# Rotated scan states in one operation, the gated product of the S5 branch in fp32, and four score banks, in a hybrid decoder block

## The chip, the cores and the metric

The kernel runs on one core of a Trainium2 chip. The metric is the device time of one execution in microseconds (us), the median over runs. The engines of the core run side by side, each through its own list of instructions in the order of that list: PE (TensorE, matrix products into PSUM banks), DVE (VectorE), ACT (ScalarE), POOL (GpSimd) and SP (SyncE, here only transfers). They wait for each other through semaphores.

## The reference

One decoder layer on 512 tokens of width 1024. The mixer in its middle has two branches, of which the change touches the second and the front of the first:

```
h = h + 1/2 * SwiGLU_1(RMSNorm(h))
z = RMSNorm(h) @ W_in      # queries, keys, values, branch gates, S5 input u
o = concat(NSA(8 heads x 64), S5(32 groups x 16 channels)) @ W_out
h = h + o
h = h + 1/2 * SwiGLU_2(RMSNorm(h))
h = h + sigmoid(RMSNorm(h) @ W_gate) * (p @ W_ple)
out = RMSNorm(h)

# S5, complex state of 64 for each group:
bu    = (u @ b) * b_coef
state = scan over time of  s[t] = a_bar * s[t-1] + bu[t]
y     = Re(state) @ c_re - Im(state) @ c_im + d_skip * u
y     = gelu(y)
out   = y * sigmoid(y @ w_glu + b_glu)

# NSA: three attentions (compressed, selected and window blocks), mixed by gates
```

## The kernel before

All data is fp32. Most matrix products are made from halves: a factor is split into a rounded part `hi` (a cast on ACT, L147) and a rest `lo` (a subtraction on DVE, L149), and three fast products `xh*hi + xl*hi + xh*lo` replace one fp32 product (`mm3`). `oh` and `ol` are the two halves of the input of `W_out`. The weights come in units of 128x1024 numbers (`raw<-in_wpack`, issued on ACT's queue into a ring of four buffers).

The program is FFN1 (to about 390 us, with `s5_constants` in the background on DVE and POOL), the mixer, and FFN2 with the last gate. In the mixer the S5 scan runs in time blocks of 8, so a group has 64 steps. It is cut into 8 chunks `j` of 4 groups (GC=4). For each chunk, `s5_in` loads the constants `sc`, multiplies the input into bank `w` (PE), turns the result by a complex rotation (L788 to L791, DVE), scans (L794), and turns the states back (L797 to L802) into `xx`, shifted by one step. `s5_out` multiplies `u` and `xx` by further constants into bank `y`, where the two groups of a pair stand at partitions 0 and 64, and ACT copies `y` out (L816). After every second chunk `s5_back` transposes eight 64-token pieces and ACT copies them to `yt` (L826). There are four `yt`, one for every 128 channels. `glu` first runs `gelu2` on each `yt` (ACT square, DVE, ACT tanh, DVE: L744 to L752) and then the product with `w_glu`.

Beside the S5 chunks stand, in the order in which a timeline simulator in the build lays them out on each engine: `scores` of query blocks 3 and 2 (16 groups each: two products and a mask into bank B, the row maximum `nmax` on DVE, the exponential on ACT), the compressed keys and values (`cmp_kv`, `cmp_all`: 32 fp32 products of width 256, `KAc`, `KBc`, `VLc`), the gates, the `glu`, `compressed(3, 2)` (the scores on compressed keys, 16 small pairs of products for each block), and the products of `out_half(4..8)` with `W_out` (96 split products) that fill gaps from there on. The hand-written part of the order is the code of the mixer's end (L1201 to L1208). After about 566 us the values phase follows, in which no line of the change stands.

The queries come through `qf` (SP's queue) as three halves: `QA` upper part (ACT, L1035), `QA` lower part (DVE, L1037), and `QB` (DVE, L1036; its rows 64 to 112 are written with zeros by an ACT cast of 1.04 us, L1039).

Of the kernel before, what the change touches and what calls it, by code (L numbers as in the profile page):

```python
# [10 lines left out]
F32 = mybir.dt.float32  # L11
# [65 lines left out]
def block_kernel(ctx: ExitStack, tc: tile.TileContext, a: dict, out: bass.AP):  # L77
# [341 lines left out]
    s5d = dram.tile([128, NG, 512], F32, tag="s5d", name="s5d")  # L419
    fd, md, gd, cd, sd = (s5d[:, :, i:j] for i, j in ((0, 128), (128, 256), (256, 384), (384, 448), (448, 512)))  # L420
    r8 = pers.tile([128, NG], F32, name="r8")

    def s5_constants(sp):
        yield 3
        if True:
# [175 lines left out]
            nc.gpsimd.dma_start(gd, gt[:, :, 1:9, :].rearrange("p g k o -> p g (k o)"))  # L601

# [86 lines left out]
    def mixer(ctx):  # L689
# [89 lines left out]

        def s5_in(j):  # L780
            sc = s5w.tile([128, GC, 512], F32, tag="sc", name="sc", bufs=3)
            G.dma_start(sc, s5d[:, GC * j:GC * j + GC])
            co, si = sc[:, :, 384:448], sc[:, :, 448:512]
            w = bank(TW, (128, GC, 64))
            for g in range(GC):
                mm(w[:, g], sc[:, g, 0:128], u8[:, GC * j + g], True, True)
            t1, t2 = (s5w.tile([128, GC, 64], F32, tag=n, name=n) for n in ("t1", "t2"))
# [8 lines left out]
            x1, x2 = (s5w.tile([128, GC, 64], F32, tag=n, name=n) for n in ("t1", "t2"))  # L796
            V.tensor_tensor(x2[64:128], vv[0:64], si[0:64], OP.mult)  # L797
            V.tensor_tensor(x2[0:64], vv[64:128], si[64:128], OP.mult)
            V.tensor_tensor(x1, vv, co, OP.mult)
            xx = s5w.tile([128, GC, 64], F32, tag="xx", name="xx")  # L800
            G.memset(xx[:, :, 0:1], 0.0)
            V.tensor_tensor(xx[:, :, 1:64], x1[:, :, 0:63], x2[:, :, 0:63], OP.add)  # L802
            return sc, xx

        def s5_out(j, yc, sc, xx):
# [12 lines left out]
        def s5_back(m, yc):  # L818
            p = bank(TP, (128, 8, 64))
            for t in range(8):  # L820
                PE.transpose(p[:, t], yc[:, t], ident[:64, :64])
# [4 lines left out]
            S.copy(yt, p.rearrange("p t c -> p (t c)"))  # L826
# [150 lines left out]

# [524 lines left out]
```

## Time and profile before

| what | value |
| --- | --- |
| median of 3 runs | 1079.37 us (1076.33 to 1081.54) |
| profiled execution | 1077.02 us, of which the span of the trace is 1075.2 us |
| granted TensorE clock, mean | 0.988 |
| busy: PE, DVE, ACT, POOL | 1038.5, 775.6, 462.3, 162.8 us |

The profiled execution is one further run, 2.35 us below the median of the three. The 1.8 us between its time and its span lie before the first and after the last instruction. Ends of matrix products are modelled, so products that follow each other closely overlap in the rows; what one costs is the distance from its start to the next start. In the rows of a timeline "x4" means four records merged; an fp32 product leaves two records.

### The profile page before, as it was taken

To read this page: it belongs to the slowest core of one execution; us is meant where nothing else is said; L and a number is where in the kernel's file an instruction comes from. 1 tells how busy PE (TensorE), PEld (TensorE's weight loads), DVE (VectorE), ACT (ScalarE), POOL (GpSimd) and SP (SyncE) were. 2 spreads that over 40 slices of the span, in tenths; PEclk is the share of its full clock that TensorE was granted. 3 is DMA by queue.
4 is the path that set the end of the run, shared out by engine and by line. 5 is a ranking of instruction groups with operands and counts; after the bars stand their busy time and mean duration, and the time that the engine had idled before them with its cause. 6 is when DMAs were issued, how large, how long until landed. Compare 5 with 4: busy or idle time off the path is not lost.

```text
span 1075.2 us, 15120 instructions
## 1 busy us (share of the span) xinstructions
PE 1038.5 (97%) x5854; PEld 879.3 (82%) x5854; DVE 775.6 (72%) x1328; ACT 462.3 (43%) x786; POOL 162.8 (15%) x187
## 2 busy tenths in 40 slices
PE   7999999999999999998899999999999999999995
PEld 5888888888888888865687667899899899898895
DVE  6995454545447857889688977996598588687766
ACT  6222223124222523346859865654255246255541
POOL 4006065425629300000000000000000000000000
PEclk9999999999999999999799999999999999999998
DMA  7333335335833837866120014333233423325402
GB/s 258 118 99 102 94 98 156 104 94 175 176 98 111 282 111 219 227 195 226 40 78 21 1 40 137 99 118 118 79 119 107 129 77 101 118 80 162 131 3 79
DMA packets 48696, 128.48 MB, mean 119 GB/s; under 512 B 10400, under 2 KB 17152, under 8 KB 47600
## 3 DMA queue, kind: packets, MB, share of 16 engines
q10 hardware_dynamic: 26080, 90.51, 27.0%
q0 software_dynamic: 4336, 17.60, 6.2%
q1 hardware_dynamic: 18208, 19.40, 5.8%
q8 instruction: 46, 0.75, 0.3%
q14 instruction: 26, 0.21, 0.1%
HBM read 111.99 MB, written 15.73 MB: 119 GB/s over the span
## 4 chain that ended last, share of the span: by engine, by line
PE 82%; DVE 8%; issue 4%; ACT 4%; DMA 2%; POOLq 0%; POOL 0%; DVEq 0%; SPq 0%; ACTq 0%
PE ps_C L126 24%; PE ps_A L126 24%; PE ps_B L126 22%; PE ps_D L126 11%; DVE nmax L1055 1%; DVE lo L149 1%; ACT e L744 1%; DMA raw<-in_wpack 1%; DMA cst<-vcd 1%; ACT eh L744 1%; ACT ps_B L744 1%; DVE el L1150 0%; ACT oh L998 0%; DVE QA L1037 0%; DVE vv L794 0%
## 5 line engine op out<-in xcount | busy, mean ns | idle before, releaser
L147 ACT CAST hi<-raw 128x1024 fp32r<-128x1024 f32 (+2 forms) x148 | 153.8, 1042 | 346.8 <-PE ps_C L126 125.0
L149 DVE TENSOR_TENSOR lo<-raw,hi 128x1024 fp32r<-128x1024 f32 (+2 forms) x148 | 191.1, 1294 | 53.4 <-ACT hi L147 52.8
L126 PE MATMUL ps_C<-hq,hi 128*128 128x512 f32 x704 | 217.3, 390 | 0.7 <-DVE h L404 0.7
L126 PEld LDWEIGHTS ps_C<-hq,hi 128*128 128x128 f32 x704 | 131.5, 188 | 28.2 <-DVE h L404 1.5
L126 PE MATMUL ps_A<-xh,hi 128*128 128x512 f32 (+1 forms) x376 | 132.6, 353 | 7.2 <-ACT xh L170 6.3
L126 PE MATMUL ps_C<-hq,lo 128*128 128x512 f32 x352 | 137.0, 389 | 0.0
L126 PE MATMUL ps_A<-xl,hi 128*128 128x512 f32 (+1 forms) x376 | 132.7, 353 | 0.9 <-DVE xl L222 0.8
L126 PE MATMUL ps_A<-xh,lo 128*128 128x512 f32 (+1 forms) x376 | 131.9, 351 | 1.7 <-DVE lo L149 1.7
L126 PE MATMUL ps_B<-xh,hi 128*128 128x512 f32 (+1 forms) x280 | 102.7, 367 | 0.9 <-ACT hi L147 0.9
L126 PE MATMUL ps_B<-xh,lo 128*128 128x512 f32 (+1 forms) x280 | 102.7, 367 | 0.0
L126 PE MATMUL ps_B<-xl,hi 128*128 128x512 f32 (+1 forms) x280 | 102.3, 365 | 0.0
L264 POOL TENSOR_TENSOR ri<-ms,negh 128x4 f32<-128x4 f32 (+1 forms) x6 | 5.5, 920 | 582.8 <-DVE ms L263 582.8
L126 PEld LDWEIGHTS ps_A<-xh,hi 128*128 128x128 f32 x376 | 71.5, 190 | 17.4 <-ACT xh L170 6.3
L404 DVE SCALAR_TENSOR_TENSOR h<-ps_C,h 128x512 f32<-128x512 f32 x64 | 43.9, 689 | 55.4 <-PE ps_C L126 55.4
L126 PEld LDWEIGHTS ps_A<-xl,hi 128*128 128x128 f32 x376 | 71.4, 190 | 12.6 <-DVE xl L222 2.4
L126 PEld LDWEIGHTS ps_A<-xh,lo 128*128 128x128 f32 x376 | 71.5, 190 | 11.0 <-DVE lo L149 1.9
L147 ACT CAST hi<-s 128x1024 fp32r<-128x1024 f32 x40 | 42.1, 1053 | 86.8 <-PE ps_D L126 37.6
L126 PEld LDWEIGHTS ps_C<-hq,lo 128*128 128x128 f32 x352 | 66.1, 188 | 13.7
L149 DVE TENSOR_TENSOR lo<-s,hi 128x1024 fp32r<-128x1024 f32 x40 | 49.0, 1225 | 16.5 <-ACT hi L147 16.4
L126 PEld LDWEIGHTS ps_B<-xh,hi 128*128 128x128 f32 x280 | 52.7, 188 | 10.0 <-ACT hi L147 1.3
L126 PEld LDWEIGHTS ps_B<-xh,lo 128*128 128x128 f32 x280 | 52.7, 188 | 9.0 <-DVE lo L149 0.4
L126 PEld LDWEIGHTS ps_B<-xl,hi 128*128 128x128 f32 x280 | 52.7, 188 | 8.7 <-issue 0.2
(402 smaller groups left out, 2311.0 us busy)
## 6 DMA issues: line engine op xcount, KB each, us to landing
raw<-in_wpack ACTq DMA_DIRECT2D x168, 512.0 KB, 3.6
sc<-s5d POOLq DMA_DIRECT2D x8, 1024.0 KB, 7.5
raw<-in_wpack SPq DMA_DIRECT2D x4, 512.0 KB, 7.3
h<-in_xT SPq DMA_DIRECT2D x8, 256.0 KB, 4.9
s5d<-fs POOLq DMA_DIRECT2D x1, 2048.0 KB, 11.6
s5d<-gt POOLq DMA_DIRECT2D x1, 2048.0 KB, 13.7
s5d<-tcs POOLq DMA_DIRECT2D x2, 1024.0 KB, 9.3
qf<-qd SPq DMA_DIRECT2D x16, 128.0 KB, 3.1
```

What stands on the lines that cost most here:

```text
L126: return PE.matmul(o, lhsT, rhs, start=start, stop=stop, **kw)
L147: S.copy(hi[:, c], raw[:, c])
L149: V.tensor_tensor(lo[:, c], raw[:, c], hi[:, c].bitcast(F32), OP.subtract)
L264: G.tensor_tensor(ri, ms, negh[:, :nb], OP.pow)
L404: V.scalar_tensor_tensor(h[:, m, :], o, 0.5, h[:, m, :], OP.mult, OP.add)
L744: S.activation(*args, **kw)
L1055: V.tensor_reduce(mc, s_, AX.X, OP.max, negate=True)
```

## The change

In `s5_in` the operations L797 to L802 (three products, a memset on POOL and one addition) become one product that writes both the cosine and the sine part of the states into `z`, of two fixed buffers whose first column is set to zero once. The exchange of halves and the sum go into `s5_out`: three products for each group instead of two, the third with constants `gs`, which are `gd` with the halves of the partitions exchanged and are written by two more stores in `s5_constants`. The constants of a chunk come in two loads (`si` 512 KB, `so` 768 KB, instead of `sc` 1024 KB). The transposes of `s5_back` write the natural token order, so later operations read in order. `glu` multiplies `yt` with the unsplit weights in fp32 and makes `oh`, `ol` only of its result. `QB` moves from DVE to ACT, the scores of block 2 use banks B and C, and `compressed(3, 2)` is written ahead of the products of `glu`.

```diff
+        zs = [s5w.tile([128, 2, GC, 64], F32, name="z", bufs=1, tag=f"z{i}") for i in range(2)]
+        for z in zs:
+            G.memset(z[:, :, :, 0:1], 0.0)
         def s5_in(j):
-            sc = s5w.tile([128, GC, 512], F32, tag="sc", name="sc", bufs=3)
-            G.dma_start(sc, s5d[:, GC * j:GC * j + GC])
+            si_ = s5w.tile([128, GC, 256], F32, tag="si", name="si", bufs=3)
+            G.dma_start(si_, s5i[:, GC * j:GC * j + GC])
+            so = s5w.tile([128, GC, 384], F32, tag="so", name="so")
+            G.dma_start(so, s5o[:, GC * j:GC * j + GC])
...
-            V.tensor_tensor(x2[64:128], vv[0:64], si[0:64], OP.mult)
-            V.tensor_tensor(x2[0:64], vv[64:128], si[64:128], OP.mult)
-            V.tensor_tensor(x1, vv, co, OP.mult)
-            xx = s5w.tile([128, GC, 64], F32, tag="xx", name="xx")
-            G.memset(xx[:, :, 0:1], 0.0)
-            V.tensor_tensor(xx[:, :, 1:64], x1[:, :, 0:63], x2[:, :, 0:63], OP.add)
-            return sc, xx
+            z = zs[j % 2]
+            cs_ = si_.rearrange("p g (a c) -> p a g c", c=64)[:, 2:4, :, 0:63]
+            V.tensor_tensor(z[:, :, :, 1:64], vv[:, None, :, 0:63].to_broadcast([128, 2, GC, 63]), cs_, OP.mult)
+            return so, z
...
-                for lhs, cols, start in ((u8[:, GC * j:GC * j + GC], slice(128, 256), True),
-                                         (xx, slice(256, 384), False)):
+                for n, lhs in enumerate((u8[:, GC * j:GC * j + GC], z[:, 0], z[:, 1])):
                     for p in range(2):
                         g = 2 * i + p
-                        mm(y[64 * p:64 * p + 64, i], lhs[:, g], sc[:, g, cols], start, not start)
+                        mm(y[64 * p:64 * p + 64, i], lhs[:, g], so[:, g, 128 * n:128 * n + 128], n == 0, n == 2)
...
                 gelu2(yt, yt, SEQ, ("r1", "r2")[m % 2])
-                S.activation(oh[:, m], yt, AF.Copy, scale=0.5)
-                V.scalar_tensor_tensor(ol[:, m], yt, 0.5, oh[:, m].bitcast(F32), OP.mult, OP.subtract)
...
-                    wu = unit()
+                    raw = unit(True)
                 o = bank("A")
                 for k in range(4):
                     q = (m * 4 + k) % 8
-                    mm3(o, wu[0][:, sl], wu[1][:, sl], oh[:, k], ol[:, k], k == 0, k == 3)
+                    mm(o, raw[:, q * 128:(q + 1) * 128], yts[k], k == 0, k == 3)
...
-                V.tensor_scalar(QB[0:64, hs], qf[0:64], 0.125, None, OP.mult)
+                S.activation(QB[0:64, hs], qf[0:64], AF.Copy, scale=0.125)
...
-        sg = chain(scores(3, envs[3], mp, TS, G3), scores(2, envs[2], mp, TS, G2))
+        sg = chain(scores(3, envs[3], mp, TS, G3), scores(2, envs[2], mp, "BC", G2))
...
         next(gg)
         drain(cg)
-        drain(gg)
+        c32 = compressed(3, 2)
+        for _ in range(2):
+            next(c32)
+            next(gg)
...
-        drain(compressed(3, 2))
+        drain(c32)
         shifts(2, 4)
+        drain(gg)
```

The order of the instructions shows the change at three places. On PE, the output products of the first chunk stand so before (`xx` the turned states, `sc` the constants):

```order
L126 MATMUL ps_C<-u_3032,sc 128x64 x2
L126 MATMUL ps_D<-sc,xx 64x128 x2
L126 MATMUL ps_D<-sc,u_3032 64x128 x2
L126 MATMUL ps_D<-sc,xx 64x128 x2
L126 MATMUL ps_C<-u_3032,sc 128x64 x2
L126 MATMUL ps_D<-sc,u_3032 64x128 x2
```

and so now:

```order
L126 MATMUL ps_A<-xl,hi 128x512
L126 MATMUL ps_D<-so,z 64x128 x4
L126 MATMUL ps_D<-so,u_3035 64x128 x2
L126 MATMUL ps_D<-so,z 64x128 x4
L126 MATMUL ps_A<-xh,lo 128x512
```

Where two products with `xx` stood for a pair of groups, four with `z` stand.

On ACT, behind the copy of the last `yt` (the end of the last `s5_back`), two `QA` and both zero casts, this stands between the square and the tanh of the last gelu before (`L744 gt<-yt` and `L744 gt<-gt`; `L981` is the split of the finished `yt`):

```order
L744 ACTIVATE gt<-yt 128x512
L972 CAST VLc<-ps_D 31x64
L744 ACTIVATE ps_B,den<-ps_B,nmax 128x384
L1035 ACTIVATE QA<-qf 128x512
L744 ACTIVATE ps_B,den<-ps_B,nmax 128x384
L972 CAST VLc<-ps_D 31x64
L1035 ACTIVATE QA<-qf 128x512
L744 ACTIVATE gt<-gt 128x512
L744 ACTIVATE ps_B,den<-ps_B,nmax 128x384
L981 ACTIVATE oh<-yt 128x512
```

and this stands there now, behind the same copy, two `QA`, two `QB` and the zero casts; the DMA row requests a weight unit of `W_out`, and `hi<-raw` splits two of them:

```order
L750 ACTIVATE gt<-yt 128x512
L750 ACTIVATE gt<-ps_A 128x256
L106 DMA raw<-in_wpack 128x1024
L750 ACTIVATE ps_B,den<-ps_B,nmax 128x384
L147 CAST hi<-raw 128x1024 x2
L1037 ACTIVATE QB<-qf 64x512
L1036 ACTIVATE QA<-qf 128x512
L1037 ACTIVATE QB<-qf 64x512
L1036 ACTIVATE QA<-qf 128x512
L750 ACTIVATE gt<-gt 128x512
L750 ACTIVATE ps_B,den<-ps_B,nmax 128x384
```

Two weight splits and two `QB` are new between the square and the tanh, as two `QB` are new ahead of the zero casts. The tanh stands behind the weight splits, and so behind whatever these wait for.

On PE, the products of the `glu` stood among the chunks and scores before:

```order
L126 MATMUL ps_A<-oh,hi 128x512
L126 MATMUL ps_A<-ol,hi 128x512
L126 MATMUL ps_B<-KA,QA 128x512
L126 MATMUL ps_B<-KB,QB 128x512
L126 LDWEIGHTS identb
L126 MATMUL ps_B<-maskq,identb 128x128
L126 MATMUL ps_A<-oh,lo 128x512
```

and now they all stand behind the last `s5_back`; three of them follow the products of the compressed keys, and the others stand here, behind the last group of scores into bank B (`ht` and `chid` belong to the compressed keys):

```order
L126 MATMUL ps_B<-KA,QA 128x384
L126 MATMUL ps_B<-KB,QB 128x384
L126 LDWEIGHTS identb
L126 MATMUL ps_B<-maskq,identb 128x128
L126 MATMUL ps_A<-yt,raw 128x512
L962 MATMUL ps_C<-ident,ht 128x128 x2
L126 MATMUL ps_A<-yt,raw 128x512 x8
L126 MATMUL ps_D<-chid,w_3010 64x63 x2
L126 MATMUL ps_D<-w_3010,chid 31x64 x2
L126 MATMUL ps_A<-yt,raw 128x512 x4
```

The first product with `yt` in this piece reads the last `yt`, which the tanh above is on the way to. Ahead of the end of the last `s5_back` there stood 18 split products of the `glu` and 7 groups of scores of block 2 before, and all 32 products of the compressed keys; now none of the `glu`, 13 groups, and 25 of the 32. By the end of `compressed(2)` PE has run 18 products of `out_half` before, and 6 now.

## Rows read from the trace of the kernel before

**Rows 1.** The page, the chain that ended last: shares of the span by engine

```profile
PE 82%; DVE 8%; issue 4%; ACT 4%; DMA 2%; POOLq 0%; POOL 0%; DVEq 0%; SPq 0%; ACTq 0%
```

**Rows 2.** Windows: width, then PE, PEld, DVE, ACT, POOL, clock, DMA, GB/s

```profile
433.00:480.00 47.00, 44.46 (x316) 35.62 (x314) 43.20 (x99) 18.01 (x39) 2.01 (x6) 1.00 0.69 207
480.00:500.00 20.00, 19.52 (x151) 12.83 (x147) 19.56 (x47) 14.09 (x32) 1.40 (x5) 1.00 0.92 320
500.00:513.70 13.70, 10.38 (x65) 6.96 (x63) 11.76 (x28) 7.43 (x20) 0.00 (x0) 0.88 0.21 66
513.70:525.25 11.55, 7.06 (x30) 4.47 (x30) 8.24 (x19) 9.90 (x25) 0.00 (x0) 0.65 0.16 45
525.25:543.30 18.05, 18.05 (x93) 14.63 (x94) 13.27 (x20) 12.77 (x24) 0.00 (x0) 0.85 0.20 59
```

**Rows 3.** Waits of PE, 433 to 513.7: us in total, times, longest

```profile
PE ps_A L126 <- ACT oh L981: 2.7, 1, 2.7
PE ps_D L126 <- DVE xx L802: 2.5, 2, 2.1
```

**Rows 4.** PE in order of time: start, us, instruction, idle before it

```profile
513.02 0.71 PE L821 MATMUL ps_D<-ident,ysb 64*128 64x64 f32 x8
...
517.41 0.69 PE L126 MATMUL ps_B<-KA,QA 128*128 128x384 f32 x1 [2.33 <-ACT ps_B L744]
...
525.25 1.22 PE L126 MATMUL ps_A<-oh,hi 128*128 128x512 f32 x2 [0.20 <-ACT oh L981]
...
543.17 0.19 PE L126 MATMUL ps_B<-cmq,identb 128*128 128x32 bf16 x1
```

**Rows 5.** DVE groups by line, 433 to 545: busy us, mean ns, idle

```profile
L999 DVE SCALAR_TENSOR_TENSOR ol<-sg,oh 128x512 fp32r<-128x512 f32 x4 | 4.3, 1086 | 1.9 <-ACT oh L998 1.9
...
L799 DVE TENSOR_TENSOR t<-vv,sc 128x256 f32<-128x256 f32 x8 | 3.4, 424 | 0.1
...
L802 DVE TENSOR_TENSOR xx<-t,t 128x252 f32<-128x252 f32 x8 | 3.3, 412 | 0.1
L1036 DVE TENSOR_SCALAR QB<-qf 64x512 fp32r<-64x512 f32 x8 | 3.2, 414 | 2.2 <-DMA qf<-qd 2.2
...
L982 DVE SCALAR_TENSOR_TENSOR ol<-yt,oh 128x512 fp32r<-128x512 f32 x4 | 2.7, 685 | 0.1
```

**Rows 6.** PE in order of time, one s5_out pair of pairs

```profile
446.93 0.39 PE L126 MATMUL ps_D<-sc,u 128*64 128x128 f32 x4
447.15 0.39 PE L126 MATMUL ps_D<-sc,xx 128*64 128x128 f32 x4
```

**Rows 7.** PE in order of time, two fp32 records among split ones

```profile
397.08 1.02 PE L126 MATMUL ps_D<-dg,ones 128*128 128x512 f32 x2
...
398.16 0.39 PE L126 MATMUL ps_B<-xh,hi 128*128 128x512 f32 x1
398.39 0.40 PE L126 MATMUL ps_B<-xl,hi 128*128 128x512 f32 x1
```

**Rows 8.** PE in order of time, two steps of cmp_all

```profile
482.10 0.38 PE L126 MATMUL ps_A<-raw,cs 128*63 128x256 f32 x1
...
482.31 0.38 PE L126 MATMUL ps_A<-raw,cs 128*63 128x256 f32 x1
```

**Rows 9.** ACT in order of time behind the last s5_back

```profile
513.87 0.58 ACT L826 COPY yt<-ps_D 128x512 f32<-128x512 f32 x1
514.34 1.16 ACT L1035 ACTIVATE QA<-qf 128x512 fp32r<-128x512 f32 x2
515.52 1.04 ACT L1039 CAST QB<-zero 48x1024 fp32r<-48x1024 f32 x1
516.59 0.56 ACT L744 ACTIVATE ps_B<-ps_B,nmax 128x384 f32<-128x384 f32 x1
```

**Rows 10.** DVE, the last operation of the last gelu2

```profile
523.84 0.69 DVE L752 SCALAR_TENSOR_TENSOR yt<-gt,yt 128x512 f32<-128x512 f32 x1
```

**Rows 11.** The page, DMA issues: count, KB each, median us to landing

```profile
raw<-in_wpack ACTq DMA_DIRECT2D x168, 512.0 KB, 3.6
```

More of the change, by code (lines that the diff above doesn't have):

```diff
@@ L415, in ffn @@
                     down(CHUNKS[i], i == len(CHUNKS) - 1)
-    s5d = dram.tile([128, NG, 512], F32, tag="s5d", name="s5d")
-    fd, md, gd, cd, sd = (s5d[:, :, i:j] for i, j in ((0, 128), (128, 256), (256, 384), (384, 448), (448, 512)))
+    s5i = dram.tile([128, NG, 256], F32, tag="s5i", name="s5i")
+    fd, cd, sd = (s5i[:, :, i:j] for i, j in ((0, 128), (128, 192), (192, 256)))
+    s5o = dram.tile([128, NG, 384], F32, tag="s5o", name="s5o")
+    md, gd, gs = (s5o[:, :, i:j] for i, j in ((0, 128), (128, 256), (256, 384)))
     r8 = pers.tile([128, NG], F32, name="r8")
@@ L601, in s5_constants @@
             nc.gpsimd.dma_start(gd, gt[:, :, 1:9, :].rearrange("p g k o -> p g (k o)"))
+            for r in (0, 64):
+                nc.gpsimd.dma_start(gs[64 - r:128 - r], gt[r:r + 64, :, 1:9, :].rearrange("p g k o -> p g (k o)"))
             yield 15
@@ L818, in s5_back @@
         def s5_back(m, yc):
-            p = bank(TP, (128, 8, 64))
+            p = bank(TP, (128, 64, 8))
             for t in range(8):
-                PE.transpose(p[:, t], yc[:, t], ident[:64, :64])
+                PE.transpose(p[:, :, t], yc[:, t], ident[:64, :64])
             if m < 2:
@@ L825, in s5_back @@
                 yt = npool.tile([128, SEQ], F32, tag=("sq", "dg")[m - 2], name="yt", bufs=1)
-            S.copy(yt, p.rearrange("p t c -> p (t c)"))
+            S.copy(yt, p.rearrange("p c t -> p (c t)"))
             yts.append(yt)
@@ L989, in glu @@
                     q = (m * 4 + k) % 8
-                    sl = slice(q * 128, (q + 1) * 128)
-                    mm3(o, wu[0][:, sl], wu[1][:, sl], oh[:, k], ol[:, k], k == 0, k == 3)
-                sg = mp.tile([128, 8, 64], F32, tag="ra", name="sg", bufs=2)
-                act(sg.rearrange("p t c -> p (t c)"), o, AF.Tanh, scale=0.5, bias=bglu[:, m:m + 1])
-                yf = yts[m].rearrange("p (t c) -> p t c", t=8)
-                V.scalar_tensor_tensor(sg, sg, 1.0, yf, OP.add, OP.mult)
-                nat = sg.rearrange("p t c -> p c t")
-                hv_ = oh[:, 4 + m].rearrange("p (c t) -> p c t", t=8)
-                S.activation(hv_, nat, AF.Copy, scale=0.25)
-                V.scalar_tensor_tensor(ol[:, 4 + m].rearrange("p (c t) -> p c t", t=8), nat, 0.25, hv_.bitcast(F32),
-                                       OP.mult, OP.subtract)
+                    mm(o, raw[:, q * 128:(q + 1) * 128], yts[k], k == 0, k == 3)
+                sg = mp.tile([128, SEQ], F32, tag="ra", name="sg", bufs=2)
+                act(sg, o, AF.Tanh, scale=0.25, bias=bglu[:, m:m + 1])
+                V.scalar_tensor_tensor(sg, sg, 1.0, yts[m], OP.add, OP.mult)
+                S.activation(oh[:, 4 + m], sg, AF.Copy, scale=0.25)
+                V.scalar_tensor_tensor(ol[:, 4 + m], sg, 0.25, oh[:, 4 + m].bitcast(F32), OP.mult, OP.subtract)
                 yield
```

9 lines of the change are left out of this document (4 added, 5 removed).

## The prediction, made before the changed kernel ran

> **What bounds the kernel now.** I read the chain that ended last first: it runs through PE for 82% of the span, DVE 8%, ACT 4% [rows 1]. PE is the bound of the kernel, so a change pays only where it takes work from PE, or idle time, or half clock. I then read windows over the stretch in which nearly all changed code lies, 433 to 543.3 us [rows 2]. The reader is to see that PE is busy 44.46 of 47.00, 19.52 of 20.00, 10.38 of 13.70, 7.06 of 11.55 and 18.05 of 18.05: 10.8 us idle. From 500 on the granted clock lies between its two levels of 1.2 and 2.4 GHz: 0.88, 0.65 and 0.85 of full, which loses 0.12 x 13.70 = 1.6, 0.35 x 7.06 = 2.5 (the busy part) and 0.15 x 18.05 = 2.7, in all 6.8 us. So 17.6 us can be got here at most. DVE is nearly full at the same time (43.20 of 47.00, 19.56 of 20.00), and names most of the waits: up to 513.7 PE waits 2.5 us for `xx` of DVE and 2.7 us for the split `oh` of ACT, which itself waits for the gelu [rows 3]. Behind it the waits of 2.33 us for the exponential and, smaller, for `oh` [rows 4] stand in ACT's order.
>
> I split the stretch at two points: T, the end of the last `s5_back` (513.02 + 0.71 = 513.7), and C, the end of `compressed(2)` (543.3) [rows 4]. Behind C both orders are alike but for twelve products of `out_half` which PE has already done before and has not done now. One costs 398.39 - 398.16 = 0.23 us [rows 7], so twelve cost 2.8. The time to beat is therefore C = 543.3 - 2.8 = 540.5.
>
> **The change, work that DVE loses.** A chunk loses three products of 0.42 and an addition of 0.41 [rows 5], 1.67 us together, and gains one product of 128x504. No row shows it. At the rate of the 128x512 form L982 it takes 0.69, at that of the strided L999 1.09 [rows 5]; I take 0.7, since only one operand is spread. Eight chunks save 7.8 us (4.6 at the other end). `QB` leaves DVE, 8 x 0.41 = 3.3. The four `ol` of `gelu` outputs go, 4 x 0.69 = 2.7, and the four others get 0.4 shorter, 1.6 [rows 5]. With two weight splits DVE loses about 18 us. None of this counts by itself: it counts as far as PE's waits get shorter.
>
> **Work that PE gains and loses up to T.** The third product of `s5_out` adds 32 products. Two of them (four records, at partitions 0 and 64) take 447.15 - 446.93 = 0.22 us [rows 6], so 16 pairs add 3.5; if the two did not go side by side, it would be up to 7. I take 3.9, for the changes of shape between neighbours. Six groups of scores come ahead of T that stood behind it: two products of 384 columns at 0.75 x 0.23 = 0.17 each and a mask, about 0.4, together +2.4. The 18 split products of the `glu` go behind T, -18 x 0.23 = -4.1. Seven products of the compressed keys go behind T, at 482.31 - 482.10 = 0.21 [rows 8], -1.5. The transposes write every eighth element instead of a row; no row shows that, and between nothing and their doubling (4 x 0.71) I take nothing, since the same number of elements is written. The net is +0.7.
>
> From T = 513.7 go the idle time up to it (2.54 + 0.48 + 3.32 = 6.3) and the half clock (1.6) [rows 2], if DVE's relief covers all waits: 513.7 - 7.9 + 0.7 = 506.5. Not all go. The last chunks wait for loads that are asked for only when a buffer is free, and one wait before is behind a transfer. I put 1.2 us on what stays (between nothing and 2.5, the part of the idle time before 480 [rows 2]). So T is 507.7, 6.0 us earlier than before.
>
> **Behind T.** If nothing waits, PE needs 7 x 0.21 for the compressed keys, 3 groups of scores 1.2, sixteen fp32 products of the `glu`, small products of `ht` and `chid` 1.2, six products of `out_half` 1.4, and `compressed` twice, 2.6. One fp32 product of 128x512 is two records: from 397.08 to 398.16 one stands with one split product, 1.08 - 0.23 = 0.85 [rows 7]. Sixteen take 13.6 us, where 48 split ones took 48 x 0.23 = 11.0. The sum is 21.5.
>
> But the order on ACT makes PE wait. With the copy of the last `yt` starting 0.2 behind T and taking 0.58 [rows 9], ACT comes to T+0.8. The two `QA` and two `QB` at 0.58 each (1.16 for two [rows 9]) end at T+3.1, both zero casts (1.04 each) at T+5.2, the exponential (0.56 and its reading, 0.7) at T+5.9. PE is through with the compressed keys at T+1.5 and its next scores wait for that exponential: idle 4.4 us. They and three fp32 products take it to T+8.9, another group of scores to T+9.3. The next group waits for an exponential that stands behind the tanh of the last gelu, and the next product of the `glu` for the end of this gelu. The tanh comes so: the two weight units are asked for at about T+5.9 and T+6.9, and a unit lands 3.6 us later [rows 11]; their casts, of 1024 columns as the zero cast, run from T+9.5 and end at T+11.6 (the second lands at T+10.5). Four more `QA` and `QB` end at T+13.9, the tanh at T+14.5, its last DVE operation (0.69 [rows 10]) at T+15.2. Before, the copy stood at 513.87 and this operation ended at 524.53, T+10.8 [rows 9, 10]. So PE is idle from T+9.3 to T+15.2, 5.9 us. Then remain 21.5 - 1.5 - 0.8 - 2.6 = 16.6 us of work. The third block of the `glu` needs a bank which ACT frees only after another weight split; I add 0.5.
>
> The clock falls in such a gap: before, one of 2.7 us lies in the stretch that loses 1.6 us, and later ones, 2.33 and less, lie in stretches that lose 2.5 and 2.7 [rows 2 to 4]. Two gaps of 4.4 and 5.9 cost between 1.6 and 5.2; I take 2.3, one recovery and a half. C is T + 15.2 + 16.6 + 0.5 + 2.3 = T + 34.6 = 542.3, against 540.5: **+1.8 us**.
>
> The Trainium skill, "TensorE: Matmul & The Clock Gate", section "Part 1: The HAM clock gate", says that the clock falls to half when PE has been idle and comes back only when it has been busy again. It speaks against this change, which joins several short gaps to two longer ones, and the trace agrees: the levels of 0.88 and 0.65 stand behind idle gaps. The price of it is taken from rows above.
>
> **Edits at nothing.** The two further stores (2 MB) in FFN1 lie beside FFN1's matrix products, hundreds of us ahead of their first use; at the 320 GB/s of [rows 2] they would cost 6.3 us if PE had to wait for them. `QB` costs ACT 8 x 0.58 = 4.6 us and saves it the four `oh` splits; ahead of T, ACT is idle for half of the time and hides this (18.01 of 47.00 busy [rows 2]). POOL's eight memsets go; it has nothing else to do. The scores in two banks let ACT and PE overlap, which is in the assumption that no wait for banks stays ahead of T.
>
> **Sum.** The profiled execution of 1077.0 would become 1078.8. It lies 2.35 below the median of the runs, 1079.37; with the same distance the median would be 1081. I say **1080.5 us**, a little less, since the waits left ahead of T are the least certain term: no change that a measurement of this kernel can tell (about 0.5%, 5.4 us).
>
> **The rivals.**
> (a) The gain comes through, 28 in 100. The weight units of `W_out` land before ACT comes to their casts, or DVE's relief lets the gelus run early, so that the last `yt` is ready when PE gets there at T+9.3. C is then T + 21.5 plus the first gap, T+25 with 1.0 us for its clock: about 532.7 to 533, and the median 1079.4 - 7.6 = 1072. For it speak the 17.6 us of idle time and lost clock [rows 2] and the 18 us that DVE loses; against it, that ACT's order is fixed, and has the casts of units that were asked for a few us before.
> (b) Slower, by the clock, 17 in 100. PE resumes at T+15.2 with three fp32 products between waits, and the clock stays at half for most of the `glu`. It decides from the point at which the granted clock between T+15 and C is as low as 0.70: 16.6 us of work then lose 7.1 instead of 2.3, and the median is 1085.5. For it speaks 0.65 behind the gaps before [rows 2], against it that the work behind T+15.2 is dense.
> (c) The loads, 10 in 100. A chunk moves 1.25 MB instead of 1, in a stretch whose DMA share is already 0.92 at 320 GB/s [rows 2]. For the five chunks loaded behind 433 that is 1.25 MB more, 3.9 us of transfers. If PE waits for all of it, T is 3.9 later and the median 1084.5. Against it: the input part is half a load and comes first.
> The Trainium skill, "Trainium Kernel Development and Optimization", section "Key Constraints", says that transfers issued from several engines share the same 16 DMA engines; by it, two loads instead of one give no more bandwidth, which is rival (c). No run here shows it yet.
> (d) The change does nothing, as PE's added work (+0.7 ahead of T, +2.6 in the `glu`) cancels the waits: that is within the forecast, 45 in 100, whose own range is 1075 to 1086.
>
> **Numbers.** The range is 1069 to 1088: it takes in most of (a), with a first gap that shrinks as well, and (b) and (c) with bounds of the gap's price, and leaves out about 17 in 100. Faster by over 0.5% is (a) but for its upper end, and the lower end of the forecast: 0.29. Slower is two thirds of (b), half of (c) and the upper end of the forecast: 0.21. The rest is 0.50.
>
> **What would show it.** In the new profile: the DVE group of `z` at about 0.7 us and no waits of PE for it; the products `so,z` in pairs of 0.22; T at about 507.7; a fp32 product each 0.85; a PE gap of 5 to 6 us ahead of the fourth product with `yt`, ended by DVE's last gelu operation; the clock low for some 5 us behind it. I am wrong if the gap is below 2 us, if T is later than 511, or if a stretch outside 433 to 543 changes its length.

## The result, and the profile after

| what | before | after |
| --- | --- | --- |
| median | 1079.37 us | 1084.75 us (1084.22 to 1087.95) |
| ratio to before | | 1.0055 [1.0031, 1.0079] |
| profiled execution | 1077.02 us | 1084.60 us |
| clock granted, mean; busy PE, DVE | 0.988; 1038.5, 775.6 | 0.990; 1044.9, 760.7 |

The changed kernel is about 5.4 us (0.5%) slower; the interval does not reach 1, so the loss is real. The forecast was 1080.5, and the range (1069 to 1088) holds the time. Yet one of the two large terms of the sum did not come at all: T, the end of the last `s5_back`, stayed where it was.

The chain that ended last of the kernel after, shares of the span by engine (before: [rows 1]):

```profile
PE 86%; ACT 4%; DVE 4%; issue 3%; DMA 3%; POOL 0%; ACTq 0%; POOLq 0%; DVEq 0%; SPq 0%
```

DVE's share has halved, from 8% to 4%: the relief of DVE is real. PE's has risen by 4 points. The windows of the kernel after, for the stretches of [rows 2] (width, then PE, PEld, DVE, ACT, POOL, clock, DMA, GB/s), say why the time did not follow:

```profile
433.00:480.00 47.00, 41.98 (x311) 33.49 (x309) 39.51 (x86) 19.09 (x41) 4.92 (x9) 0.96 0.84 250
480.00:500.00 20.00, 20.00 (x156) 15.47 (x153) 17.11 (x42) 12.90 (x36) 1.08 (x2) 1.00 0.27 81
500.00:513.70 13.70, 13.70 (x111) 8.60 (x110) 6.61 (x16) 7.71 (x23) 0.00 (x0) 1.00 0.53 180
513.70:525.25 11.55, 6.54 (x30) 3.15 (x29) 6.67 (x11) 10.13 (x18) 0.00 (x0) 0.96 0.68 200
525.25:543.30 18.05, 15.85 (x45) 7.57 (x46) 8.74 (x15) 8.99 (x20) 0.00 (x0) 0.84 0.39 118
```

From 480 to 513.7 everything went as planned: PE is busy for all of 33.70 us, at full clock, where it was idle for 3.8 us before. But from 433 to 480 it is idle for 47.00 - 41.98 = 5.02 us, against 2.54 [rows 2], and from 513.7 on for 5.01 + 2.20. I call idle time plus the busy time that a clock below full loses the **lost time** of a stretch. Before it is 7.6 us up to 513.7 and 9.7 from there to 543.3, 17.2 in all (the prediction's 17.6 counts the clock of 500 to 513.7 over the whole 13.70 us instead of the busy 10.38); after it is 5.02 + 0.04 x 41.98 = 6.7 and 5.01 + 2.20 + 0.04 x 6.54 + 0.16 x 15.85 = 10.0, together 16.7. So the change got back half a microsecond of lost time and added 6.0 us of work for PE: from 433 to C (546.0, row below) less the lost time are 113.0 - 16.7 = 96.3 us, where before 107.5 - 17.2 = 90.3 stood up to the 540.5 to beat. The prediction had 3.9 for the third product of `s5_out` and 2.6 for the fp32 ones.

The waits of PE after, 433 to 560 (us in total, times, longest; before: [rows 3, 4]):

```profile
PE ps_A L126 <- DVE yt L758: 6.1, 1, 6.1
PE ps_B L126 <- ACT ps_B L750: 4.6, 4, 3.1
PE ps_B L126 <- DVE QA L1038: 1.0, 1, 1.0
PE ps_D L126 <- DVE z L811: 0.5, 1, 0.5
```

The waits for `xx` and for the split `oh` are gone. In PE's order of time the larger ones, and the work behind them, are (start, us, instruction, idle before it):

```profile
465.17 0.50 PE L126 MATMUL ps_B<-KA,QA 128*128 128x512 f32 x1 [3.08 <-ACT ps_B L750]
...
513.27 0.46 PE L829 MATMUL ps_D<-ident,ysb 64*128 64x64 f32 x4
...
520.64 0.45 PE L126 MATMUL ps_B<-KA,QA 128*128 128x384 f32 x1 [0.66 <-ACT ps_B L750]
...
527.45 2.08 PE L126 MATMUL ps_A<-yt,raw 128*128 128x512 f32 x2 [6.11 <-DVE yt L758]
529.32 0.63 PE L962 MATMUL ps_C<-ident,ht 128*128 128x128 f32 x2
529.75 7.75 PE L126 MATMUL ps_A<-yt,raw 128*128 128x512 f32 x16
537.42 0.45 PE L126 MATMUL ps_D<-chid,w 128*64 128x63 f32 x4
...
538.14 3.70 PE L126 MATMUL ps_A<-yt,raw 128*128 128x512 f32 x8
541.27 0.79 PE L126 MATMUL ps_A<-oh,hi 128*128 128x512 f32 x1
...
545.98 0.19 PE L126 MATMUL ps_B<-cmq,identb 128*128 128x32 bf16 x1
```

T is 513.27 + 0.46 = 513.7, as before [rows 4]; `compressed(2)` ends at C = 546.0, against the 540.5 that were to be beaten. The +5.5 pass through: the values phase begins at 572.62 instead of 566.91, and FFN2's first product with `hq` at 746.86 instead of 738.87. The last 2.3 us of the second difference arise in the values phase, in which no line of the change stands. Its windows 30 to 70 us behind its start, before and after:

```profile
597.00:637.00 40.00, 38.01 (x154) 24.79 (x154) 34.10 (x73) 30.71 (x62) 0.00 (x0) 1.00 0.04 14
```

```profile
603.00:643.00 40.00, 38.16 (x149) 25.20 (x149) 33.78 (x74) 30.82 (x62) 0.00 (x0) 0.96 0.05 14
```

The clock takes 0.04 x 38.16 = 1.5 us there in this one execution. The profiled execution of before lies 2.35 us below its median and that of after at its median, so 5.5 is nearer to what the change costs than the 7.6 between the two.

**Where the early wait comes from.** POOL, the queue that requests the chunks' constants, in order of time, before:

```profile
447.66 0.11 POOL L801 MEMSET xx<- 128x4 f32 x1 [56.61 <-PE ps_D L126]
448.17 0.62 POOL L782 DMA_DIRECT2D sc<-s5d  x1 [0.41 <-issue]
```

and after:

```profile
440.37 0.62 POOL L793 DMA_DIRECT2D si<-s5i  x1 [49.26 <-PE ps_C L126]
445.01 0.54 POOL L795 DMA_DIRECT2D so<-s5o  x1 [4.03 <-PE ps_D L126]
453.65 0.54 POOL L793 DMA_DIRECT2D si<-s5i  x1 [8.10 <-DVE z L811]
```

Before, POOL sat at the memset of `xx` until the output products of chunk 0 (`ps_D`) were done, and only then asked for chunk 3. But it was not the memset that held the request: `sc` has three buffers, so chunk 3 takes that of chunk 0, which the same output products read until 447.15 + 0.39 = 447.54 [rows 6]. Without the memset the request could have come some 0.6 us earlier. After, the input part has three buffers of its own, which no output product reads. The last reader of chunk 0's, by the code, is its product `z` on DVE:

```profile
439.15 0.68 DVE L811 TENSOR_TENSOR z<-vv,si 128x504 f32<-128x504 f32 x1
```

The profile puts the wait of this request down to the input products, which end at 440.33, and that of the four later ones to `z`. So it is the split of the load that lets the request come 7.8 us earlier; no run takes the memset away alone. The queries are on their way just then, from 438.3 on (SP's queue). Their transfers from 430 to 470, time to landing, minimum, median and maximum, before and after:

```profile
DMA to landing us min/median/max: 2.6/3.3/8.3
```

```profile
DMA to landing us min/median/max: 3.6/6.9/9.2
```

And ACT, in order of time: before, the first query is taken at 443.88,

```profile
443.88 0.63 ACT L1035 ACTIVATE QA<-qf 128x512 fp32r<-128x512 f32 x1 [2.68 <-DMA qf<-qd]
```

and after, at 446.88, and a later one, with an exponential behind it, at 463.17:

```profile
446.88 0.63 ACT L1037 ACTIVATE QB<-qf 64x512 fp32r<-64x512 f32 x1 [6.70 <-DMA qf<-qd]
...
463.17 0.63 ACT L1037 ACTIVATE QB<-qf 64x512 fp32r<-64x512 f32 x1 [4.40 <-DMA qf<-qd]
463.70 0.61 ACT L1036 ACTIVATE QA<-qf 128x512 fp32r<-128x512 f32 x1
464.34 0.66 ACT L750 ACTIVATE ps_B<-ps_B,nmax 128x512 f32<-128x512 f32 x1
```

The exponential at 464.34 is the one for which PE waits until 465.17. ACT was idle for 4.40 us with it in its list, behind a `QB` whose query had not landed. The row maximum that it needs was ready at 461.69, so ACT's order held it for 2.65 us:

```profile
461.00 0.69 DVE L1056 TENSOR_REDUCE nmax<-ps_B 128x1 f32<-128x512 f32 x1
```

This query is not one of those that were under way at 440. SP asked for it at 454.61, behind `vcd`, where before it asked at 449.55 ahead of `vcd`; beside it run the loads requested at 453.65 and 455.11. The early request of chunk 3 reaches this gap through the delay of the first queries. The Trainium skill, "PSUM — Partial Sum Buffer", section "Engine vs sequencer instructions", says that ScalarE's queue is strictly first in, first out; the trace agrees, with these 2.65 us.

**The late wait.** ACT behind the last transposes, after:

```profile
513.76 0.59 ACT L834 COPY yt<-ps_D 128x512 f32<-128x512 f32 x1 [0.30 <-PE ps_D L829]
...
520.48 1.04 ACT L147 CAST hi<-raw 128x1024 fp32r<-128x1024 f32 x1
522.82 1.04 ACT L147 CAST hi<-raw 128x1024 fp32r<-128x1024 f32 x1 [1.29 <-DMA raw<-in_wpack]
523.77 0.62 ACT L1037 ACTIVATE QB<-qf 64x512 fp32r<-64x512 f32 x1
...
525.86 0.61 ACT L750 ACTIVATE gt<-gt 128x512 f32<-128x512 f32 x1
```

and DVE's last operation of this gelu:

```profile
526.70 0.69 DVE L758 SCALAR_TENSOR_TENSOR yt<-gt,yt 128x512 f32<-128x512 f32 x1
```

The tanh of the last gelu (525.86) stands behind two weight splits, one of which waits 1.29 us for its unit, and four `QA` and `QB`; DVE's operation follows at 526.70, 12.9 us behind the start of the copy (before 523.84 - 513.87 = 10.0 [rows 9, 10]).

### The profile page after: what moved, and what is told of

It is laid out like the page before. It is cut to its first block, busy times and chain, and to the rows that moved or that the text cites. A ratio compares the mean times of both kernels' runs of the same rounds, so it can differ in the third digit from the quotient of the medians.

```text
span 1082.8 us, 15177 instructions
## 1 busy us (share of the span) xinstructions
PE 1044.9 (97%) x5902; PEld 880.0 (81%) x5902; DVE 760.7 (70%) x1290; ACT 460.7 (43%) x788; POOL 169.4 (16%) x191
## 4 chain that ended last, share of the span: by engine, by line
PE 86%; ACT 4%; DVE 4%; issue 3%; DMA 3%; POOL 0%; ACTq 0%; POOLq 0%; DVEq 0%; SPq 0%
PE ps_A L126 27%; PE ps_C L126 25%; PE ps_B L126 22%; PE ps_D L126 11%; DMA qf<-qd 1%; ACT e L750 1%; DMA raw<-in_wpack 1%; DVE lo L149 1%; ACT eh L750 1%; ACT ps_B L750 1%; DVE el L1151 0%; DMA qd<-r 0%; ACT hi L147 0%; PE ps_D L589 0%; ACT pt L1157 0%
## 5 line engine op out<-in xcount | busy, mean ns | idle before, releaser
L149 DVE TENSOR_TENSOR lo<-raw,hi 128x1024 fp32r<-128x1024 f32 (+2 forms) x146 | 188.7, 1296 | 53.6 <-ACT hi L147 53.0
L126 PEld LDWEIGHTS ps_A<-xh,hi 128*128 128x128 f32 x376 | 71.6, 190 | 16.7 <-ACT xh L170 6.2
L126 PEld LDWEIGHTS ps_C<-hq,lo 128*128 128x128 f32 x352 | 66.1, 188 | 13.7
```

The source lines that it names most:

```text
L126: return PE.matmul(o, lhsT, rhs, start=start, stop=stop, **kw)
L149: V.tensor_tensor(lo[:, c], raw[:, c], hi[:, c].bitcast(F32), OP.subtract)
```

## The experiments

The theories. **L (loads):** the early lost time comes from the constants of chunk 3, which are asked for earlier and run beside the queries' transfers. **Q (queries on ACT):** it comes from `QB` on ACT, whose wait blocks the exponentials behind it. **F (tail):** the late wait comes from the weight splits ahead of the last tanh on ACT. **W (work):** the added work of PE alone makes the kernel slower, above all the fp32 product. All versions compute the whole reference. e5, e6 and e11 start from the kernel before, the others from the changed one. The kernel before had medians of 1078.1 to 1079.4 beside them, so versions are compared by the ratio. In this table lost time is that of the five windows in one profiled execution (17.2 before, 16.7 after):

| version | ratio to before | median us | T | lost up to 480 | lost 433 to 543 |
| --- | --- | --- | --- | --- | --- |
| e1 `QB` on DVE | 1.0054 [1.0037, 1.0071] | 1085.74 | 516.1 | 9.7 | 18.6 |
| e2 chunk 3 later | 1.0028 [1.0014, 1.0042] | 1083.48 | 509.6 | 2.9 | 11.7 |
| e3 splits behind the tanh | 1.0020 [1.0008, 1.0032] | 1081.79 | 513.8 | 6.4 | 13.5 |
| e4 e1 and e3 | 1.0003 [0.9988, 1.0018] | 1079.72 | 514.1 | 5.2 | 10.5 |
| e5 S5 part alone | 1.0031 [1.0015, 1.0046] | 1082.59 | 506.8 | 5.8 | 12.3 |
| e6 `glu` alone | 1.0102 [1.0081, 1.0122] | 1090.89 | 516.5 | 2.6 | 18.2 |
| e7 e2 and e3 | 0.9998 [0.9983, 1.0012] | 1079.28 | 510.4 | 3.4 | 8.5 |
| e8 e7 and e1 | 1.0005 [0.9993, 1.0018] | 1079.52 | 515.8 | 8.3 | 13.1 |
| e9 e7, queries later on ACT | 1.0018 [1.0005, 1.0032] | 1079.67 | 512.1 | 5.3 | 14.5 |
| e10 e9 and e1 | 1.0012 [0.9995, 1.0028] | 1080.68 | 513.1 | 6.2 | 15.6 |
| e11 e5, chunk 3 later | 1.0022 [1.0006, 1.0037] | 1081.07 | 503.4 | 4.5 | 12.9 |
| e12 `glu` split as before | 1.0074 [1.0054, 1.0095] | 1086.53 | 514.9 | 7.3 | 19.8 |

Executions of one version spread over 3 to 8 us, so a single trace shows where it waits, and the ratio what that is worth. T is compared only between versions with the same order of work; in e5, e6, e11 and e12 other work stands ahead of it.

**e1: `QB` back on DVE.**

```diff
-                S.activation(QB[0:64, hs], qf[0:64], AF.Copy, scale=0.125)
+                V.tensor_scalar(QB[0:64, hs], qf[0:64], 0.125, None, OP.mult)
```

> QB back on DVE, all else as changed. Theory Q (ACT's order: the QB operations stand on ACT ahead of QA and wait there for the query transfers, and exponentials, QA and through them the scan stand behind): the idle time of PE from 433 to 480 falls from 5.0 us to 2.6 or less, the end of the last transposes comes from 513.7 to 509 to 511, and the wait for the last yt shortens from 6.1 to 4 to 5 us, since two QB fewer stand ahead of the tanh; in all 1079 to 1081 us. Theory L (the constants of a chunk are asked for earlier and in more bytes, and delay the query transfers whoever reads them): DVE waits for the same transfers instead, PE idles 4 to 5 us there as now, and the time stays at 1083 to 1085 us.

No gain. PE's idle time up to 480 did fall, from 5.02 to 3.07 us, and the wait behind `QB` went. In its place PE waited for a chunk's constants. The wait of PE, and the windows 460 to 480:

```profile
PE ps_C L126 <- DMA si<-s5i: 2.5, 1, 2.5
```

```profile
460.00:470.00 10.00, 7.82 (x44) 6.30 (x45) 6.76 (x16) 3.95 (x11) 0.54 (x1) 0.60 0.97 262
470.00:480.00 10.00, 10.00 (x66) 8.21 (x66) 8.59 (x22) 3.91 (x10) 1.61 (x3) 0.72 0.46 146
```

Behind that one gap of 2.5 us the clock was at 0.60 and 0.72, so this execution lost 9.7 us up to 480, more than the 6.7 of the changed kernel. Q names a true wait, but taking it away alone does not gain: another wait for a transfer took its place.

**e2: chunk 3's constants asked for only when the second pair of queries has landed.** A copy of one column on POOL waits for it, ahead of the request.

```diff
-            G.dma_start(si_, s5i[:, GC * j:GC * j + GC])
+            if j == 3:
+                kick = s5w.tile([64, 1], F32, name="kick", bufs=1)
+                g_ = G.tensor_copy(kick, qfs[1][0:64, 0, 0:1])
+            with tc.issue_after(g_.ins) if j == 3 else nullcontext():
+                G.dma_start(si_, s5i[:, GC * j:GC * j + GC])
```

> The fourth chunk's constants (and what follows on POOL's queue) are asked for only when the second query transfer of block 3 has landed; QB stays on ACT. Theory L: the queries land near 444 as before the change instead of 446.9, ACT's wait of 6.7 us shrinks to about 3.7, PE's idle time up to 480 falls by 2 to 3 us, and the time to 1081 to 1083. Theory Q: the landing moves by less than 1 us, PE's idle time stays within 1 us of 5.0, and the time at 1084 to 1086; if the chunks' constants then come too late for the input products, up to 1087.

POOL and, below, PE of this version in order of time, and its first window:

```profile
445.38 0.35 POOL L795 COPY kick<-qf 64x1 f32<-64x1 f32 x1 [54.26 <-DMA qf<-qd]
445.89 0.63 POOL L797 DMA_DIRECT2D si<-s5i  x1 [0.16 <-issue]
```

```profile
452.04 1.07 PE L126 MATMUL ps_C<-u,si 128*128 128x64 f32 x8 [1.45 <-DMA si<-s5i]
```

```profile
433.00:480.00 47.00, 44.10 (x339) 35.63 (x338) 41.81 (x92) 21.42 (x48) 5.83 (x11) 1.00 0.88 266
```

With the request 5.5 us later the first `QB` begins at 443.14 instead of 446.88, the long wait for the exponential is gone, the clock stays at 1.00, and T is 4.1 us earlier. The 1.45 us that PE now waits for these constants are the price. So in this order L is right on where the early time was lost. Over all executions the gain is smaller: 1.0028 against 1.0055 is 2.9 us, and by medians it is 1.3; the two intervals overlap. The profiled execution (1079.41) is the shortest of its twelve, which reach to 1084.84; the gain does not come in each.

**e3: the splits of the first weight units of `W_out` behind the last tanh.**

```diff
-            act(t, t, AF.Tanh, scale=math.sqrt(2 / math.pi) * 0.044715)
+            with tc.issue_after(table[0].ins):
+                tanhs.append(S.activation(t, t, AF.Tanh, scale=math.sqrt(2 / math.pi) * 0.044715))
...
-                        wu = unit()
+                        with tc.issue_after(last) if last else nullcontext():
+                            wu = unit()
```

> The weight splits of the output product stand on ACT behind the tanh of the last gelu; all else as changed, and PE's order there is the same. Theory T (the wait of 6.1 us for the last yt is ACT's order, of which the splits and the landing they wait for are half): the tanh starts near 522.5 instead of 525.86, the wait falls to about 3 us, and the time by 3 to 4 us, to about 1081. Rival: the splits come late for the output products, or the queries of block 0 wait as long as the splits did; then the time is within 1 us of 1084.75. The idle time up to 480 stays at 5.0 us by all theories.

The wait for the last `yt` fell from 6.11 to 2.83 us and the median by 3.0 (3.8 us by the ratio), with T unchanged. PE's wait and ACT's tanh, now 3.2 us earlier:

```profile
PE ps_A L126 <- DVE yt L759: 2.8, 1, 2.8
```

```profile
522.64 0.62 ACT L758 ACTIVATE gt<-gt 128x512 f32<-128x512 f32 x1
```

F is shown, with its size; the same edit takes 0.0051 from the ratio of e1 (e4). What is left of the wait is the `QA`, `QB`, zero casts and exponentials ahead of the same tanh.

**e4 (e1 and e3), e7 (e2 and e3), e8 (all three).** The edits are those above, together.

> Both edits. Theories Q and T: the gains add, since they lie in different stretches, and the last four QB are gone from ACT ahead of the tanh too: 1076 to 1078 us, faster than before the change by 0.1 to 0.3%. Theory L with T: 1080 to 1081. If both theories fail: 1084 to 1085.

> Both the delayed request of the fourth chunk's constants and the weight splits behind the last tanh; QB stays on ACT. If the two act in different stretches, their effects of -1.3 and -3.0 us add: 1080 to 1081. By theory L in full (the first wait is worth the 4.1 us by which the transposes came earlier in the profiled execution with the delayed request), 1077 to 1078. If the clock decides by chance which of the executions gains, the median stays at 1081 to 1082.

> The same with QB on DVE. Theory Q (QB on ACT costs as soon as the transfers are on time and nothing waits for constants): 2 us faster than the one with QB on ACT, 1075 to 1078. By what the single edits gave (QB alone -0 to +1, with the splits -2): 1078 to 1080. If DVE's own wait for the queries or the constants of the third chunk takes the place: 1080 to 1082.

All three come to the time of before: 1.0003, 0.9998, 1.0005. e2 and e3 alone take 0.0027 and 0.0035 from 1.0055; together (e7) they take 0.0057, clear of the intervals, so their effects add, as two separate places should. e7's windows have the least lost time of all versions (from 480 to 513.7 and from 525.25 on PE is full, at clock 1.00):

```profile
433.00:480.00 47.00, 45.38 (x335) 36.72 (x333) 40.97 (x90) 20.79 (x45) 5.82 (x11) 0.96 0.87 259
...
513.70:525.25 11.55, 7.63 (x19) 3.42 (x18) 7.43 (x12) 10.46 (x22) 0.00 (x0) 0.85 0.46 140
```

Why `QB` on DVE gains beside e3 (e4) and not alone (e1) is not settled; the sum of e1's and e3's effects, 1.0019, lies just outside e4's interval, so it may be chance.

Neither L nor Q is the whole of the early loss. The twelve versions with the split load fall into four groups of three; the numbers are the idle time of PE up to 480, one execution each:

| | `QB` on ACT | `QB` on DVE |
| --- | --- | --- |
| chunk 3 asked for early | changed 5.0, e3 4.8, e12 4.3 | e1 3.1, e4 3.5, e5 4.9 |
| chunk 3 asked for later | e2 2.9, e7 1.6, e9 2.2 | e8 7.1, e10 4.5, e11 4.5 |

In all six with the early request ACT takes its first query at 446.3 to 447.4, in all six with the later one at 443.1 to 445.5, and at 443.9 to 444.0 with the old loads (before, e6). That is L. But the gap of 3.0 to 3.2 us at 465 stands only in the three versions which also have `QB` on ACT. The later request takes 0.0027 (e2) and 0.0022 (e7 against e3) from the ratio where `QB` is on ACT; where it is on DVE, e8 against e4 and e11 against e5 show no gain clear of their intervals, and PE waits for exponentials instead (1.7 to 5.3 us).

**e5: before with the S5 part alone (one product for the turned states, three output products, two loads); e6: before with the `glu` part alone (fp32 product, natural order).** In both `QB` is on DVE, block 2 in bank B, and `compressed` behind the `glu`, as before. Of e5, against the changed kernel:

```diff
-                    raw = unit(True)
+                    wu = unit()
...
-                    mm(o, raw[:, q * 128:(q + 1) * 128], yts[k], k == 0, k == 3)
+                    mm3(o, wu[0][:, sl], wu[1][:, sl], oh[:, k], ol[:, k], k == 0, k == 3)
```

and of e6:

```diff
-            V.tensor_tensor(z[:, :, :, 1:64], vv[:, None, :, 0:63].to_broadcast([128, 2, GC, 63]), cs_, OP.mult)
+            V.tensor_tensor(x2[64:128], vv[0:64], si[0:64], OP.mult)
...
+            V.tensor_tensor(xx[:, :, 1:64], x1[:, :, 0:63], x2[:, :, 0:63], OP.add)
```

> The kernel before with the S5 part of the change alone (one product for the rotated states, three products per group in the output, two loads per chunk, two more stores); the gelu, the product of the S5 branch, QB, banks and order as before. Theory L (more and earlier constants hold up the other small transfers of this stretch): query or rotation-table transfers land 2 to 5 us later than before the change, PE idles 4 us or more from 433 to 480 where it idled 2.5, and with 3.9 us more work on PE the time is 1081 to 1085 us. Rival (the S5 part is sound and its DVE relief pays; the loss is the rest of the change): PE's idle time up to 513 falls from 6.3 to 3 us or less, and the time is 1075 to 1079.

> The kernel before with the fp32 product of the S5 branch and the natural token order alone. Sixteen fp32 products take 13.6 us where 48 split ones took 11.0, so 2.6 us more for PE if nothing else moves. Theory T (the late part of the change pays only by order): the splits of yt are gone from the chain behind the last transposes, its end comes 1 to 2 us earlier, and the time is within 2 us of 1079.4. Rival (the fp32 products are what slows the changed kernel): 1082 or more, with the same idle time as before the change.

The S5 part alone costs 3.3 us, the `glu` part alone 11. They do not add up to the whole (5.9 by its ratio): the build lays the whole order out anew for each version. e5 has the early loss without any `QB` on ACT: chunk 3 is asked for at 440.45, ACT waits 9.0 us for queries, PE is idle for 4.94 up to 480. So an early loss does not need `QB` on ACT; but it lies in other places, 1.6 us for `si` and 2.7 for an exponential at 477, not in the gap at 465. Its T is early, but from 545 to 575 it loses 6.5 us more (2.68 idle, clock 0.86), where the kernel before loses 0.8. e6 has the old loads and the old request, and no more early loss than before (2.61 us idle, as before); its waits lie later (exponentials 3.6, `KBc` 2.8, `yt` 2.6; before 3.5, 1.4 and, for `oh`, 2.9) with clocks of 0.77 to 0.83, and from 545 to 600 it loses 8.3 us where the kernel before loses 1.7. So the early loss goes with the S5 part. The time of e6 is as its rival said (1082 or more), but e12 below does not find the fp32 products at fault in the whole change; what slows e6 was not separated from its order.

**e11: e5 with e2's later request.** The edit is that of e2.

> The S5 part alone, with the fourth chunk's constants asked for only when the second query transfer of block 3 has landed. Theory L: the query transfers land near 444 as before the change, ACT's wait of 9.0 us for queries falls to about 5, PE's idle time from 433 to 480 falls from 4.9 to 3 us or less, and the time falls by 1.5 to 3 us, to 1079.5 to 1081. Rival (the requests only happen to stand beside the waits): within 1 us of 1082.6.

1.0022 against 1.0031, in the direction of L and within the intervals. The first query was taken at 444.31 instead of 447.21, as L said, but PE's idle time up to 480 fell only from 4.94 to 4.51, where 3 or less was expected. T came 3.4 us earlier (503.4), and a wait of 4.2 us for the rest of a weight split (`lo`, DVE) took most of it back.

**e9, e10: e7 with the queries and zero casts of blocks 1 and 0 behind the last tanh and the last exponentials, with `QB` on ACT and on DVE.**

```diff
-                S.activation(QA[:, hs], qf, AF.Copy, scale=0.125)
-                S.activation(QB[0:64, hs], qf[0:64], AF.Copy, scale=0.125)
+                with late():
+                    S.activation(QA[:, hs], qf, AF.Copy, scale=0.125)
+                with late():
+                    S.activation(QB[0:64, hs], qf[0:64], AF.Copy, scale=0.125)
...
+            def late():
+                st_ = ExitStack()
+                if qb < 2:
+                    st_.enter_context(tc.issue_after(tanhs[-1].ins))
+                    st_.enter_context(tc.issue_after(marks[0].ins))
+                return st_
```

(`marks[0]` is the last exponential of block 2, which the first weight units of `W_out` now follow too; a step of the `glu` is also moved by a line of the hand-written order.)

> As the run with the delayed request and the splits behind the tanh, and on ACT also all query operations of blocks 1 and 0 and both zero casts behind the last tanh and the last exponentials of block 2. Theory T: the last yt is ready about 4.5 us behind the last transposes, before PE comes to it; PE's wait of 2.8 us for it and the 1.1 us for exponentials go, and with them some of the half clock. 1075 to 1077 us, faster than before the change by 0.2 to 0.4%. Rival: the tanh of the output product of the S5 branch now stands behind these query operations, and PE waits 3 us or more for its bank: 1079 to 1080, no gain.

> The same with QB on DVE: ACT has four QB fewer ahead of the tanh of the output product. If ACT's order behind the last transposes is what still binds, 1 us faster than with QB on ACT, 1074 to 1076. If DVE's wait for the queries in the early part is worse, as the profiled execution of the last such run had it (7.1 us idle on PE up to 480 against 1.6), 1077 to 1080.

The wait for the last `yt` is gone, and nothing is gained. The waits of PE in e9, and the window behind:

```profile
PE ps_D L126 <- DVE KBc L979: 3.6, 1, 3.6
PE ps_C L126 <- DMA si<-s5i: 2.2, 1, 2.2
PE ps_D L126 <- ACT chid L969: 1.4, 1, 1.4
```

```profile
525.25:543.30 18.05, 14.41 (x54) 9.06 (x54) 14.25 (x33) 10.08 (x21) 0.00 (x0) 0.72 0.39 127
```

PE comes to the compressed keys earlier and waits there instead: `chid` now stands behind the queries and zero casts on ACT, `KBc` behind queries and weight splits on ACT and DVE. In e10 it is an exponential, for 4.5 us, and the same window is at 0.72 too.

**e12: the changed kernel with the `glu` split as before** (and with the old token order that belongs to it; the edit is the one shown of e5).

> The changed kernel with the split product of the S5 branch and the old token order back, all else as changed; PE's order up to the last transposes stays as changed. If the fp32 products cost what they take more on PE, 13.6 against 11.0 us, and the wait for the last yt stays at 5 to 7 us: 1082 to 1083 us. Rival (the split of the last yt on ACT and DVE lengthens the same wait by as much as the products get shorter): 1084 to 1086. The transposes end at 513 to 515 either way.

1.0074, so taking the fp32 product out gains nothing: the split product costs 2.6 us less on PE, and the kernel is not faster, by medians 1.8 us slower. And e7 carries all of W's added work and comes to the time of before, so the work can be paid for. The four `oh` and `ol` come back into ACT's and DVE's lists, and the wait behind them is `PE ps_C L962 <- DVE ht L758: 4.9`. The intervals of both overlap, so that it is worse is not shown.

## Why the prediction was right in its number and wrong in a step

The forecast for C was +1.8 us, as -6.0 up to T and +7.8 behind it. Measured: +5.5, as 0.0 and +5.5. That the time lies in the range is partly luck: the 6.0 us that were missed ahead of T were offset by 2.3 us less behind it, and the range is 19 us wide. By the prediction's own sign, T later than 511, it was wrong. Step by step:

- **DVE's relief: right.** The product `z` takes 0.68 us (predicted 0.7). DVE's group of it:

```profile
L811 DVE TENSOR_TENSOR z<-vv,si 128x504 f32<-128x504 f32 x8 | 5.5, 682 | 0.2
```

  From 433 to 513.7 DVE is busy for 63.2 us instead of 74.5 [rows 2], and PE's waits for `xx` and `oh` went, as said.
- **PE's added work: right.** The output products come in pairs of 0.22:

```profile
506.89 0.39 PE L126 MATMUL ps_D<-so,u 128*64 128x128 f32 x4
507.11 0.61 PE L126 MATMUL ps_D<-so,z 128*64 128x128 f32 x8
```

  and four fp32 products take 541.27 - 538.14 = 3.1, 0.78 each (predicted 0.85); the eight ahead of them, with the clock not yet full, 0.96. Without lost time the way to T has grown by 0.9 us (predicted 0.7), and that from T to C takes 32.3 - 10.0 = 22.3 (predicted 21.5).
- **The waits that stay ahead of T: the step that failed.** The prediction put 1.2 us on them, "between nothing and 2.5", and no lost clock. Measured 5.02 us idle and 1.7 of clock, 6.7 in all. This is what kept T at 513.7. Rival (c), the loads, had the right place but the wrong mechanism: it priced more bytes (3.9 us of transfers) and counted in the change's favour that the input part, half a load, comes first. It does come first, and that is the harm: it is asked for 7.8 us earlier than the old load, beside the queries, which then land late. The prediction knew that a load is asked for when a buffer is free; it did not work out when the new buffers of the input part come free, nor what is under way then. And `QB` on ACT was costed by ACT's idle time alone (4.6 us, "hides this"); that it stands ahead of exponentials and waits there for a transfer was left out. How much of the 6.7 us goes with the request is only bounded: e2's trace says 6.7 - 2.9 = 3.8, the ratios 2.9 (e2) and 2.4 (e7 against e3), the median of e2 1.3, and with `QB` on DVE the ratios of e5 and e11 say 1.0.
- **The Trainium skill**, "DMA: Bandwidth & Descriptors", section "Issuing engines are not separate DMA queues", says that transfers issued by different engines run on the same 16 DMA engines and interleave. The trace agrees: the queries are on SP's queue, the constants on POOL's, and the queries' median time to landing went from 3.3 to 6.9 us, and to 5.5 in e2.
- **The wait for the last `yt`: right**, 6.11 us against 5.9, by the mechanism given (e3 takes 3.3 of it away by moving the weight splits). PE came to the wait at T+7.6 instead of T+9.3, and the last operation of the gelu ended at 526.70 + 0.69, T+13.7 instead of T+15.2.
- **The first gap of 4.4 us: did not come.** The products of the compressed keys and three fp32 products stood ready in PE's list, and waits of 0.44 and 0.66 remained. So 10.0 us were lost behind T, where the prediction had 4.4 + 5.9 + 0.5 + 2.3 = 13.1.
- **The clock behind T**: 2.8 us lost (predicted 2.3).
- **Rival (b)**, the clock low for most of the `glu`, did not come: 0.84 in that stretch, not 0.70. **Rival (a)** would have needed both waits gone, and its sum is short: T + 21.5 with the first gap of 4.4 us as worked out and 1.0 for the clock is T + 26.9, where it has T + 25; e7 comes nearest, and has only the time of before.

So the change trades 6 us of new work on PE against lost time, and the lost time hardly fell. No version here beats the kernel before; e7 and e4 equal it, with the work paid for by less lost time. The change, or either of its two main parts, is not worth having in the forms tried. That the last waits can't be had at once is seen in e9, e10 and e11: behind each wait taken away PE met the next one.

Open: why one gap is followed by a long stretch of low clock and another not (below), and why e2's executions spread over 5 us, which their mean granted clocks (0.988 to 0.991) do not follow.

## What to carry to other kernels

In this kernel a load is asked for when the last reader of its buffer is done, so the buffers also space the transfers. When a load is split, find the last reader of each part's buffer, work out when the request will now go out, and see whose transfers are under way at that moment: the traffic at that earlier time is part of the price. When an operation that waits for a transfer moves to another engine, look at what stands behind it there. Where the bound engine gets more work in exchange for shorter waits, count the waits that are left, place by place, in the new order; behind each stands another.

## What the runs showed of the hardware

A gap of PE can cost more through the clock than by itself, and not always the same. In e1 one of 2.54 us at 462 was followed by windows at 0.60 and 0.72 of the full clock: 0.40 x 7.82 + 0.28 x 10.00 = 5.9 us. In the changed kernel one of 3.08 us at 465 left 0.83 over 460 to 470, with 6.92 us busy, and 1.00 over the next 10: 1.2 us. What PE does behind the gap differs between the two, but no run separates that from chance.
